# Where the pieces of the conditioning weights live during the attention: one in a place of its own, three in the turn of the projection weights

## The chip, the cores and the metric

The kernel runs on one core of one Trainium2 chip. The metric is the device time of one execution in microseconds (us). Engines are named as in the profile: PE is the matrix engine (PEld its weight loads), DVE the vector engine, ACT the scalar engine, SP the engine that issues nearly all transfers (SPq is its queue of issues). A tile of on-chip memory is named by its region: R, HL, H, I, O, P, Q, E.

## The reference, cut to what matters

Two decoder layers. Each is conditioned on a vector c: a row of 3072 numbers per layer (shift, scale and gate) comes from one product of a vector with a matrix, `ada_w`. Layer 0 has an attention over dilated windows beside a state-space part; layer 1 is a gated DeltaNet.

```python
c_act = jax.nn.silu(c)
for layer in range(DEPTH):
    mod = c_act @ ada_w[layer] + ada_b[layer]          # 1024 x 3072
    shift, scale, gate = jnp.split(mod, 3, axis=-1)
    h = rms_norm(x, pre_g[layer]) * (1.0 + scale) + shift
    y = ab_mixer(h, ...) if layer % 2 == 0 else gdn_mixer(h, ...)
    x = x + gate * rms_norm(y, post_g[layer])
...
# ab_mixer: z = h @ w_in, split into q, k, v, u, gate; attention(q, k, v) and s5(u);
#           (concatenation * silu(gate)) @ w_out
```

## The kernel before, in words

The sequence of 1024 rows stays on the chip; weights are streamed from memory in pieces of 512 KB (4 KB on each of 128 partitions). A framework of tiles inserts every wait. The part up to the end of the attention is written inside a block whose instructions a scheduler orders by a simulated timeline; from then on each engine keeps that order, so an instruction that waits holds all behind it on its engine.

The attention goes through four passes of two heads each (p = 0 to 3), each pass through eight tiles of 128 queries (t = 0 to 7). For a tile, PE makes the scores (L925, and L930 for the far keys), DVE adds the bias and finds the extremum (L943, L945, L948), ACT takes the exponential (L950), DVE divides (L951, L952), PE transposes (L965, L968, L971), ACT and DVE copy the transposes out (L966, L969, L972), and PE multiplies with the values (L978; L993 for the far keys, whose result DVE takes at L999). Between the tiles stands other work, the fillers:

- the projections of the next pass and of the gates. `load_w` takes one of three places of 4 KB, `RAW`, for a weight (SP, L291, 512 KB), splits it into a high part (ACT, L293) and a low part (DVE, L294), and 48 matmuls (L300) follow. The place comes free when the low part is made. The eight loads of the output weights (`wo`, from `ab_w_out`) go the same way in the last pass;
- eight calls of `ada`, each of which makes 512 of the numbers of `mod`. Its weight comes in four pieces of 512 KB (SP, L257), each with two matmuls (L261; the trace has two records for each). Then ACT copies the sum out to a tile `rt` (L264), PE turns it in four transposes (L246), and DVE adds up (L248, L265).

Two `ada` stand in each pass, named here by layer and column block: (0,4) and (0,5), (1,2) and (1,3), (1,0) and (1,1), (1,4) and (1,5). Before the change the pieces turn through the same three places of `RAW`, but with a counter of their own (`ada_p2`), so the first and the fourth piece of one `ada` share a place: the fourth transfer cannot be issued before the matmuls of the first have read it. `rt` lies in region E, in a pair of 2 KB places (`TMP`) that nothing else uses in the attention. `GT` is a pair of 2 KB places in P and Q that hold the tanh of a gate (ACT, L874) until DVE has used it (L876, L878).

The attention ends with the last L999; then comes the output projection of layer 0 (DVE and ACT prepare it from L1064 and L1065 on, PE multiplies at L1077).

## Time and profile before

| | |
|---|---|
| median of 3 runs | 1318.27 us (1317.27 to 1318.78) |
| profiled execution | 1327.74 us, its span 1326.0 us |
| mean granted clock of PE in it | 0.979 of full speed |
| PE busy | 94% of the span; DVE 68%, ACT 38% |
| attention in the trace | 229 to 541.5 us |

PE is busy nearly throughout, so what can be gained or lost in the attention is the time in which PE sits idle there, and the time in which its clock is granted only half. Those are read from the timeline of PE, where the idle time in front of a group of instructions stands in brackets with what ended it. The profiled execution is 9.5 us above the median of the runs.

### The profile page before, as it was taken

What the parts mean: (1) busy time and instruction counts of PE and PEld (TensorE: products, weight loads), DVE (VectorE), ACT (ScalarE), POOL (GpSimd) and SP (SyncE); (2) the same over time, 40 slices, a digit from 0 to 9 for tenths busy, and PEclk for the clock granted to TensorE, in tenths of its full rate; (3) what the DMA queues carried; (4) which work ended last, traced back from release to release, by engine and by line L of the source; (5) the groups of instructions that cost most, each with busy time, mean ns of one, the idle gap of its engine ahead of it and who ended that gap; (6) DMA issues with size and microseconds to landing.
All of it is one profiled execution on the core that took longest, in us unless ns stands there. A gap on an engine that the chain in (4) does not pass through costs nothing.

```text
span 1326.0 us, 21572 instructions
## 1 busy us (share of the span) xinstructions
PE 1241.4 (94%) x7980; PEld 952.4 (72%) x7980; DVE 903.0 (68%) x2746; ACT 505.7 (38%) x1142; POOL 23.9 (2%) x24
## 2 busy tenths in 40 slices
PE   5699999999999997899998999899999999998997
PEld 3488887856757663688765877777787778776786
DVE  7678944145252447377756978988778978988863
ACT  5462123234232335265552344423433353435421
POOL 0000000000000000000300000000000000000000
PEclk9899999999999998999998999999999999999999
DMA  9735455345051245124211122132133315255222
GB/s 315 199 93 123 121 135 158 82 120 140 0 165 55 80 124 186 69 96 133 76 32 41 48 65 81 55 88 58 57 103 81 88 48 136 76 148 182 98 87 80
DMA packets 183984, 136.62 MB, mean 103 GB/s; under 512 B 65008, under 2 KB 161629, under 8 KB 183878
## 3 DMA queue, kind: packets, MB, share of 16 engines
q1 hardware_dynamic: 167212, 124.47, 32.3%
q10 hardware_dynamic: 16586, 10.54, 2.9%
q8 instruction: 63, 1.03, 0.3%
q14 instruction: 43, 0.35, 0.1%
q0 software_dynamic: 80, 0.23, 0.0%
HBM read 107.42 MB, written 27.78 MB: 102 GB/s over the span
## 4 chain that ended last, share of the span: by engine, by line
PE 81%; DMA 7%; DVE 7%; ACT 2%; SPq 2%; issue 1%; DVEq 0%; ACTq 0%
PE psum L1275 25%; PE psum L300 14%; PE psum L1077 12%; PE psum L784 3%; PE psum L1738 2%; PE psum L1719 2%; DMA I_float<-ada_w 2%; PE psum L261 2%; PE psum L833 2%; DMA R_float<-ab_w_in 1%; DMA R_float<-ada_w 1%; PE psum L763 1%; PE psum L669 1%; DVE O_float L1305 1%; PE psum L1540 1%; PE psum L925 1%
## 5 line engine op out<-in xcount | busy, mean ns | idle before, releaser
L1275 PE MATMUL psum<-Q_float32r,HL_float32r 128*128 128x512 f32 x768 | 216.5, 416 | 6.4 <-DVE O_float L1305 3.8
L1275 PE MATMUL psum<-P_float32r,HL_float32r 128*128 128x512 f32 x768 | 210.1, 410 | 3.2 <-DVE O_float L1565 2.7
L1275 PEld LDWEIGHTS psum<-Q_float32r,HL_float32r 128*128 128x128 f32 x768 | 141.7, 194 | 37.3 <-issue 8.3
L1275 PEld LDWEIGHTS psum<-P_float32r,HL_float32r 128*128 128x128 f32 x768 | 140.7, 192 | 30.9 <-issue 3.8
L1305 DVE SCALAR_TENSOR_TENSOR O_float<-psum,vt,O_float 128x511 f32<-128x511 f32 x144 | 106.6, 740 | 1.1
L300 PE MATMUL psum<-H_float32r,HL_float32r 128*128 128x512 f32 x408 | 100.7, 397 | 2.9 <-ACT HL_float32r L293 2.9
L300 PE MATMUL psum<-I_float32r,HL_float32r 128*128 128x512 f32 x408 | 101.4, 397 | 0.0
L300 PEld LDWEIGHTS psum<-H_float32r,HL_float32r 128*128 128x128 f32 x408 | 74.9, 188 | 20.1 <-ACT HL_float32r L293 3.5
L300 PEld LDWEIGHTS psum<-I_float32r,HL_float32r 128*128 128x128 f32 x408 | 74.7, 188 | 16.9 <-issue 2.1
L1734 ACT ACTIVATE O_float<-psum,R_float 64x128 f32<-64x128 f32 x120 | 43.5, 363 | 57.2 <-DVE O_float L1725 52.9
L1310 ACT ACTIVATE E_float<-O_float 128x512 f32<-128x512 f32 x48 | 30.2, 630 | 74.1 <-DVE O_float L1305 68.6
L1077 PE MATMUL psum<-P_float32r,Q_float32r 128*128 128x512 f32 x192 | 51.9, 401 | 0.2 <-DVE Q_float32r L1065 0.2
L1756 ACT ACTIVATE O_float<-I_float 128x128 f32<-128x128 f32 x64 | 19.6, 306 | 79.9 <-DVE I_float L1755 62.3
L294 DVE TENSOR_TENSOR HL_float32r<-R_float,HL_float32r 128x1024 fp32r<-128x1024 f32 x25 | 30.5, 1221 | 28.5 <-ACT HL_float32r L293 28.4
L1725 DVE SCALAR_TENSOR_TENSOR O_float<-psum,R_float,I_float 64x128 f32<-64x128 f32 x120 | 41.7, 348 | 11.6 <-PE psum L1719 9.7
L1747 DVE SCALAR_TENSOR_TENSOR O_float<-O_float,R_float,psum 128x128 f32<-128x128 f32 x112 | 37.6, 343 | 16.4 <-PE psum L1738 9.1
L1077 PE MATMUL psum<-H_float32r,I_float32r 128*128 128x512 f32 x192 | 46.7, 390 | 1.3 <-DVE I_float32r L1065 1.3
L1738 PEld LDWEIGHTS psum<-O_float,I_float 128*128 128x128 f32 x240 | 34.4, 194 | 18.1 <-ACT O_float L1730 14.9
L1719 PEld LDWEIGHTS psum<-O_float,H_float 128*128 128x128 f32 x240 | 39.0, 193 | 10.0 <-DVE O_float L1747 2.8
L1296 ACT ACTIVATE O_float<-psum,vt 128x512 f32<-128x512 f32 x48 | 32.5, 678 | 35.7 <-PE psum L1275 35.6
L1719 PE MATMUL psum<-O_float,H_float 128*128 128x128 f32 x240 | 44.7, 288 | 1.1 <-DVE O_float L1747 1.0
L1738 PE MATMUL psum<-O_float,I_float 128*128 128x128 f32 x240 | 41.5, 294 | 3.7 <-ACT O_float L1730 3.4
(355 smaller groups left out, 2339.4 us busy)
## 6 DMA issues: line engine op xcount, KB each, us to landing
R_float<-ada_w SPq DMA_DIRECT2D x32, 512.0 KB
R_float<-gdn_w_in SPq DMA_DIRECT2D x29, 512.0 KB
R_float<-ab_w_in SPq DMA_DIRECT2D x21, 512.0 KB
I_float<-ada_w SPq DMA_DIRECT2D x8, 1024.0 KB
O_float<-x SPq DMA_DIRECT2D x8, 512.0 KB
R_float<-y_scr SPq DMA_DIRECT2D x8, 512.0 KB
R_float<-ab_w_out SPq DMA_DIRECT2D x8, 512.0 KB
R_float<-x SPq DMA_DIRECT2D x8, 512.0 KB
```

The costliest lines, as they stand in the source:

```text
L294: lo_eng.tensor_tensor(out=wh[:, 1024:2048], in0=wr, in1=wh[:, 0:1024].bitcast(F32), op=ALU.subtract)
L300: T.matmul(pj, lhsT=wh[:, sw, k, :], rhs=hT[half][:, k, sh, :], start=(k == 0 and i == 0), stop=(k == 7 and i == 2))
L784: T.matmul(pj[:, 0:256], lhsT=h4[:, k, sh_, c0:c0 + 128], rhs=wv[k // 4][:, sw, k % 4, :], start=(k == 0 and i == 0), stop=(k == 7 and i = ...
L1077: T.matmul(pb, lhsT=hl[:, so, k, :], rhs=wo[k][:, sw, 0, sl], start=(j == 0 and i == 0), stop=(j == 7 and i == 2))
L1275: T.matmul(pj, lhsT=wh[:, sw, k, :], rhs=hT[half][:, k, sh_, :], start=(n == 0), stop=(n == 23))
L1296: S.activation(t_["a"], pj, AF.Copy, scale=col("conv", 72 + b))
L1305: V.scalar_tensor_tensor(out=t_["a"][:, sl], in0=src, scalar=col("conv", 24 * i + b), in1=t_["a"][:, sl], op0=ALU.mult, op1=ALU.add)
L1719: T.matmul(psk[:, 128 * hp:128 * hp + 128], rhs=st[:, hp, :], lhsT=kq[:, c, 2 - 2 * hp:4 - 2 * hp, :].rearrange("p s i -> p (s i)"))
L1725: V.scalar_tensor_tensor(out=rt[rows], in0=psk[rows, 128 * hp:128 * hp + 128], scalar=cl["ngc"][rows, c:c + 1], in1=vc[rows], op0=ALU.mult ...
L1734: S.activation(qs[rows], psk[rows, 128 * hp:128 * hp + 128], AF.Copy, scale=egs[rows, 16 * p + c:16 * p + c + 1])
L1738: T.matmul(psu[hp], lhsT=kd[:, c % 8, hp, :], rhs=vn)
L1747: V.scalar_tensor_tensor(out=sn[:, hp, :], in0=st[:, hp, :], scalar=dec[:, hp, 16 * p + c:16 * p + c + 1], in1=psu[hp], op0=ALU.mult, op1= ...
```

## The change: what it does

The first piece of each `ada` gets region E, 4 KB, for itself. The pieces two to four are taken from `RAW` itself, by the same counter as the weights of `load_w`. Since E is taken, `rt` moves from `TMP` to the pair `GT`. No instruction is added or removed.

```diff
@@ ada
-        rt = TMP()
+        rt = GT()
         S.activation(rt, pr, AF.Copy)
...
     tables()
-    ada_p2 = Turn([p_.rearrange("p (k n) -> p k n", k=2) for p_ in RAW.places])
+    ADA_FIRST = piece(E0, 2, 512)
+    ada_i = [0]
+
+    def ada_p2():
+
+        ada_i[0] += 1
+        return RAW().rearrange("p (k n) -> p k n", k=2) if ada_i[0] % 4 != 1 else ADA_FIRST
```

The scheduler makes another order of it; the lines behind the change count seven higher. Three places.

On SP, around the start of the last pass's two `ada`. The rows with R_float<-ada_w are pieces of 512 KB, those with ab_w_out the output weights wo2 to wo7. Before:

```order
246 L257 DMA R_float_66<-ada_w 128x2x512 [waits DMAHW3_49,PE_49]
247 L291 DMA R_float_66<-ab_w_out 128x1024 [waits DMAHW2_49,PE_49]
248 L291 DMA R_float_66<-ab_w_out 128x1024 [waits DMAHW5_49,PE_49]
249 L291 DMA R_float_66<-ab_w_out 128x1024 [waits DMAHW6_49,DMAHW1_49,PE_49]
250 L291 DMA R_float_66<-ab_w_out 128x1024 [waits DMAHW7_49,DVE_49]
251 L291 DMA R_float_66<-ab_w_out 128x1024 [waits DMAHW0_49,DVE_49]
252 L291 DMA R_float_66<-ab_w_out 128x1024 [waits DMAHW4_49,DMAHW1_49,DVE_49]
253 L257 DMA R_float_66<-ada_w 128x2x512 [waits DMAHW2_49,DVE_49]
254 L257 DMA R_float_66<-ada_w 128x2x512 [waits DMAHW3_49,DVE_49]
255 L257 DMA R_float_66<-ada_w 128x2x512 [waits DMAHW4_49,DVE_49]
256 L257 DMA R_float_66<-ada_w 128x2x512 [waits DMAHW5_49,PE_49]
```

With the change:

```order
247 L257 DMA E_float_73<-ada_w 128x2x512 [waits PE_49]
248 L291 DMA R_float_66<-ab_w_out 128x1024 [waits DMAHW3_49,PE_49]
249 L291 DMA R_float_66<-ab_w_out 128x1024 [waits DMAHW6_49,PE_49]
250 L291 DMA R_float_66<-ab_w_out 128x1024 [waits DMAHW4_49,DMAHW2_49,PE_49]
251 L291 DMA R_float_66<-ab_w_out 128x1024 [waits DMAHW0_49,DVE_49]
252 L291 DMA R_float_66<-ab_w_out 128x1024 [waits DMAHW1_49,DVE_49]
253 L291 DMA R_float_66<-ab_w_out 128x1024 [waits DMAHW5_49,DMAHW2_49,DVE_49]
254 L257 DMA R_float_66<-ada_w 128x2x512 [waits DMAHW3_49,DVE_49]
255 L257 DMA R_float_66<-ada_w 128x2x512 [waits DMAHW7_49,DMAHW4_49,DVE_49]
256 L257 DMA R_float_66<-ada_w 128x2x512 [waits DMAHW5_49,DVE_49]
```

Where the fourth piece of (1,4) stood there is now the first piece of (1,5), in E, and behind the output weights stand three pieces instead of four; none of them waits for PE any more, only for DVE's low parts.

On PE, around the `ada` (1,3) of the second pass. Before:

```order
285 L261 MATMUL psum<-R_float_66,ca 32x512 x6
286 L925 MATMUL psum<-P_float_71 128x128 x2
287 L965 MATMUL psum<-cst,Q_float_1883 128x128 x4
288 L925 MATMUL psum<-P_float_71 128x256 x2
289 L968 MATMUL psum<-cst,Q_float_1883 128x128
290 L261 MATMUL psum<-R_float_66,ca 32x512 x2
291 L968 MATMUL psum<-cst,Q_float_1883 128x128
292 L978 MATMUL psum<-Q_float_1883 64x128 x4
```

With the change:

```order
291 L300 MATMUL psum<-I_float32r,HL_float32r 128x512 x2
292 L261 MATMUL psum<-E_float_73,ca 32x512 x2
293 L261 MATMUL psum<-R_float_66,ca 32x512 x6
294 L925 MATMUL psum<-P_float_71 128x128 x2
295 L971 MATMUL psum<-cst,Q_float_1883 32x128 x2
296 L246 MATMUL psum<-cst,Q_float_1883 128x128 x4
297 L925 MATMUL psum<-P_float_71 128x256 x2
298 L965 MATMUL psum<-cst,Q_float_1883 128x128 x4
```

Six matmuls, some attention and two matmuls have become one block of eight. The other five `ada` of the first three passes look the same. On SP, in front of the projection weights that follow such an `ada`, the fourth piece has given way to the first piece of the next `ada`, in E; and by their addresses in memory the weights come in another order: behind (1,3) the order was gate, q, k and is now q, k, gate, behind (0,5) it was k, gate, q and is now q, k, gate. PE multiplies with q first.

On ACT, in the last pass, from the copy of (1,4)'s sum on: L293 makes the high parts of the output weights, L966 and L950 belong to the attention's tiles t = 4 and on. Before:

```order
234 L264 ACTIVATE E_float_73<-psum 128x512
235 L966 ACTIVATE Q_float_1883<-psum 128x256
236 L293 ACTIVATE H_float32r<-R_float_66 128x1024 x2
237 L950 ACTIVATE Q_float_1883,mn<-Q_float_1883,mn 128x384
238 L966 ACTIVATE Q_float_1883<-psum 128x256 x2
239 L293 ACTIVATE H_float32r<-R_float_66 128x1024
```

With the change:

```order
237 L966 ACTIVATE Q_float_1883<-psum 128x256
238 L293 ACTIVATE H_float32r<-R_float_66 128x1024 x3
239 L966 ACTIVATE Q_float_1883<-psum 128x256 x2
240 L950 ACTIVATE Q_float_1883,mn<-Q_float_1883,mn 128x384
241 L293 ACTIVATE H_float32r<-R_float_66 128x1024
```

The high part of a third output weight (wo4) now stands ahead of the attention's two copies of the next tile.

## Rows read from the trace of the kernel before

**Rows 1.** The page: busy times, and the chain that ended last.

```profile
span 1326.0 us, 21572 instructions
PE 1241.4 (94%) x7980; PEld 952.4 (72%) x7980; DVE 903.0 (68%) x2746; ACT 505.7 (38%) x1142; POOL 23.9 (2%) x24
PE 81%; DMA 7%; DVE 7%; ACT 2%; SPq 2%; issue 1%; DVEq 0%; ACTq 0%
```

**Rows 2.** The attention, its end: length, busy PE PEld DVE ACT POOL, clock, DMA share, GB/s.

```profile
229.00:541.50 312.50, 294.07 (x2016) 195.55 (x2014) 134.26 (x499) 103.06 (x257) 0.00 (x0) 0.98 0.36 105
501.00:541.50 40.50, 30.34 (x257) 14.09 (x255) 25.45 (x92) 19.45 (x44) 0.00 (x0) 0.87 0.53 169
```

**Rows 3.** Waits of SP's queue, 215 to 545 us: total, times, longest.

```profile
SPq L257 <- PE psum L261: 135.4, 8, 40.9
```

**Rows 4.** PE's timeline, first three passes: start, length, group, idle time before it.

```profile
290.32 0.73 PE L300 MATMUL psum<-H_float32r,HL_float32r 128*128 128x512 f32 x2 [0.51 <-ACT HL_float32r L293]
...
313.35 1.05 PE L261 MATMUL psum<-R_float,ca 128*32 128x512 f32 x4 [1.63 <-DMA R_float<-ada_w]
...
316.69 0.70 PE L925 MATMUL psum<-P_float 64*128 64x256 f32 x4 [0.63 <-DVE mn L948]
...
370.12 0.66 PE L246 MATMUL psum<-cst,E_float 128*128 128x128 f32 x4 [0.22 <-ACT E_float L264]
...
385.80 1.91 PE L261 MATMUL psum<-R_float,ca 128*32 128x512 f32 x12
...
390.77 1.05 PE L261 MATMUL psum<-R_float,ca 128*32 128x512 f32 x4 [1.06 <-DMA R_float<-ada_w]
...
396.79 0.73 PE L300 MATMUL psum<-H_float32r,HL_float32r 128*128 128x512 f32 x2 [1.02 <-ACT HL_float32r L293]
...
439.70 1.91 PE L261 MATMUL psum<-R_float,ca 128*32 128x512 f32 x12
...
445.06 1.05 PE L261 MATMUL psum<-R_float,ca 128*32 128x512 f32 x4 [0.29 <-DMA R_float<-ada_w]
...
447.91 1.06 PE L300 MATMUL psum<-H_float32r,HL_float32r 128*128 128x512 f32 x2 [1.32 <-ACT HL_float32r L293]
...
469.90 1.05 PE L261 MATMUL psum<-R_float,ca 128*32 128x512 f32 x4 [0.92 <-DMA R_float<-ada_w]
```

**Rows 5.** SP's issues beside `ada` (1,3) and beside (1,0).

```profile
386.89 0.37 SPq L257 DMA_DIRECT2D R_float<-ada_w  x1
387.37 4.86 SPq L291 DMA_DIRECT2D R_float<-ab_w_in  x3
440.80 0.37 SPq L257 DMA_DIRECT2D R_float<-ada_w  x1
441.26 0.42 SPq L291 DMA_DIRECT2D R_float<-ab_w_in  x1
```

**Rows 6.** PE's timeline, last pass: groups behind a wait.

```profile
507.72 1.05 PE L261 MATMUL psum<-R_float,ca 128*32 128x512 f32 x4 [1.45 <-DMA R_float<-ada_w]
...
520.58 0.47 PE L968 MATMUL psum<-cst,Q_float 128*128 128x128 f32 x1 [3.01 <-ACT Q_float L966]
...
532.77 1.30 PE L261 MATMUL psum<-R_float,ca 128*32 128x512 f32 x4 [3.19 <-DMA R_float<-ada_w]
```

**Rows 7.** The chain from 500 to 543 us: start, length, what.

```profile
514.52 4.66 DMA R_float<-ab_w_out
...
527.78 4.95 DMA R_float<-ada_w
```

**Rows 8.** Stretches of the last pass, columns as in group 2.

```profile
510.00:520.00 10.00, 5.60 (x66) 3.21 (x66) 9.56 (x31) 6.23 (x11) 0.00 (x0) 0.99 0.62 205
520.00:522.00 2.00, 1.42 (x5) 1.01 (x7) 1.43 (x2) 1.42 (x3) 0.00 (x0) 0.50 0.71 224
```

**Rows 9.** ACT's timeline, last pass: high parts of wo4 and wo7.

```profile
513.47 1.05 ACT L293 ACTIVATE H_float32r<-R_float 128x1024 fp32r<-128x1024 f32 x1
...
521.11 1.06 ACT L293 ACTIVATE I_float32r<-R_float 128x1024 fp32r<-128x1024 f32 x1 [0.58 <-DMA R_float<-ab_w_out]
```

## The prediction

> **What bounds the kernel now.** I read the page first: PE is busy 94% of the span, and 81% of the chain that ended last is PE's own work, 7% transfers [rows 1]. So the whole kernel is bound by PE, and an edit that moves no work off PE can gain only where PE sits idle. The change touches the attention alone, so next come the stages: in the attention PE is busy 294.07 of 312.50 us, which leaves 18.4 us idle, and 10.2 of these lie in the last 40.5 us, where the clock is also lowest, 0.87 in the mean [rows 2]. Then who is waited for. In SP's queue the eight issues of an `ada` piece that wait for the matmuls of an earlier piece stand first, 135.4 us in sum [rows 3]. That is no loss by itself, since SP has nothing better to do; it says that a place comes free late. PE's timeline shows where it hurts. Each `ada` starts with three pieces present, and the fourth is issued only when the first has been read. PE fills the time with attention, and where that runs out it waits: 1.63, 1.06, 0.29 and 0.92 us in the first three passes [rows 4], 1.45 and 3.19 in the last [rows 6]. Behind these come waits for the high part of the next projection weight, 0.51, 1.02 and 1.32, and an after-effect of 0.63 through DVE [rows 4]. The last pass is another regime: from 510 to 520 us DVE is busy 9.56 of 10 us while PE does 5.60, and just after it PE's granted clock is 0.50, the 1.2 GHz level [rows 8].
>
> **The change part by part.** Work added or removed: none, the same transfers, matmuls and copies. `rt` in `GT` instead of `TMP` is the same copy; it could delay the next tanh of a gate by having the place still occupied, but two places turn and the transposes that free it follow within a few attention groups; the nearest row, a transposition that waited for the copy, is 0.22 us [rows 4]. I take 0, with 0 to 1 us for all eight.
>
> *The second `ada` of passes 0 to 2* ((0,5), (1,3), (1,1)). Now all four pieces have places before the `ada` starts, because the last one needs only a low part that DVE made long before. The wait for the fourth piece goes: 1.63, 1.06 and 0.92, and the after-effect 0.63. What is late next is the projection weight. Take (1,3): it starts at 385.80; the fourth piece went out at 386.89 and the first weights from 387.37 [rows 4, 5]. With the change the piece in E goes out at the same point, since it too waits for the first piece's matmuls, and the weights follow at A + 1.57 as before (A is the start of the `ada`). How long do they take? At (1,0) a weight was issued at 441.26 behind a fourth piece at 440.80 [rows 5]; its L300 starts at 447.91, straight after a high part of 1.06 us [rows 4, 9], so it landed near 446.8, 5.5 us after issue. With that the weight of (1,3) lands at A + 7.1 and its high part is ready at A + 8.2. PE's own work up to L300 there is 396.79 - 385.80 less the two waits of 1.06 and 1.02, so 8.9 us. It fits: both waits go, provided that the weight that PE wants comes first, and the new order has q first where the old one had the gate's. At (1,1) likewise. At (0,5) PE's new order reaches L300 earlier, after about 7.5 us by adding up its groups, an estimate, so some 0.7 us come back. Gain: 1.63 + 0.63 + 1.06 + 1.02 + 0.92 - 0.7 = 4.6 us; bounds 2 (weights some 1 us later at each) and 5.3 (no wait comes back).
>
> *The first `ada`* ((0,4), (1,2), (1,0)). Before, three pieces and a late fourth also; the waits are 0.51 at (0,4), 0.22 at (1,2), and 0.29 + 1.32 at (1,0) [rows 4]: 2.3 us. At (1,0) L300 came at 447.91 - 439.70 = 8.2 us after the start, of which 1.6 were waits, so 6.6 of work. In the new order the four transposes L246, 0.66 us, stand ahead of L300: 7.3 of work against the same 8.2 for piece in E and weight. Wait 0.95. At (1,2) the same sum with somewhat more attention gives 0.5; at (0,4) the new order has less cover, about 6.9 us, and I take 1.3. Sum 2.75: a loss of 0.45 us. Bounds: a gain of 2.3, a loss of 3.
>
> *The last pass*, counted on the chain. Before, the fourth piece of (1,5) is issued at 527.78, lands after 4.95 us [rows 7], PE starts on it at 532.77 after 3.19 us of nothing [rows 6], and the attention ends at 541.5, 8.7 us later [rows 2]. Now the three pieces in R wait only for the low parts of wo5, wo6 and wo7. The last of these: high part from 521.11 for 1.06 [rows 9], low part about as long again, so 523.3. The last piece goes out then and not at 527.78: 4.5 us earlier. It lands at 528.2, and the same 8.7 us end at 537. Some of what stands before it moves too: the wait of 1.45 for the fourth piece of (1,4) goes, since that piece is issued ahead of need. But that opens onto the stretch that DVE fills (9.56 of 10), so I give it only 0.5. Against it stands the order on ACT: the high part of wo4 stands ahead of the two copies of tile 4, and those of wo6 and wo7 ahead of tile 5's. wo4's starts at 513.47, wo7's at 521.11, so a copy may come a high part (1.06) later, twice; I do not count it in the chain, because the pieces' places hang on just these weights and come no later for it. Sum: 5.0 us gained; bounds 0 (DVE and the output weights' transfers, 4.66 us each [rows 7], fix the end) and 9 (most of the 10.2 idle us).
>
> *Start of the attention.* The first piece in E is issued ahead of the small transfer for the bias tables. Its region has been read by then, so no new wait; a share of the bandwidth: 0.5 us lost, 0 to 1.
>
> *Output projection of layer 0.* Its order changes slightly on every engine, by no change of work; PE has its matmuls in hand there. 0, within 2 either way.
>
> Sum: -4.6 + 0.45 - 5.0 + 0.5 = -8.65 us. The durations come from the profiled execution of 1327.74 us, which is 9.5 above the median of the runs, 1318.27; I take the difference over unscaled: 1318.27 - 8.65 = **1309.6 us**.
>
> **A rule weighed against it.** Near the last pair the transfers run at 169 GB/s in the mean, and at 205 from 510 to 520 [rows 2, 8], so 524 KB occupy them some 2.6 us. The Trainium skill, page "DMA: Bandwidth & Descriptors", section "Issuing engines are not separate DMA queues", says that all transfers end up on the same 16 engines and interleave. By that rule a piece in a place of its own brings no bandwidth of its own, and put ahead of a weight it only makes the weight later; the trace agrees that weights behind a piece take longer than the piece itself (5.5 against 3.9 us). By the rule alone the sum would be that of the third rival below; by the rows it is not, because a piece stood at the same spot before.
>
> **The rivals.** *The last pass gives nothing.* DVE's 9.56 of 10 us and the chain of output weights fix when the attention can end; the piece comes earlier and PE waits at L966's copies instead, as it did for 3.01 us at 520.58 [rows 6]. For it: that wait is as long as the one that goes. Against: the 3.19 us stand at the end, when DVE is nearly done. Then -4.6 + 0.45 + 0.5 = -3.65, 1314.6 us.
>
> *Nothing is gained.* Every wait for the fourth piece turns into one for the next weight, the cover being shorter now that the eight matmuls stand in a block, and the last pass gives its gain back at the weights' high parts ahead of the attention on ACT. 1318 us, within 2.6.
>
> *Slower: the piece in E holds up the weights.* If it truly comes on top, each of the six blocks in passes 0 to 2 waits 2.6 us at L300: 15.6, less the 7.6 that these passes wait now (5.3 + 2.3), and the last pass and the start still give 4.5: +3.5, 1321.8 us. It decides once the wait is above (7.6 + 4.5 + 2.6)/6 = 2.45 us per block. Against it: the fourth piece was issued at 386.89, 0.5 us ahead of the weights [rows 5], so one piece is replaced by one. For it: the cover is 7 to 9 us, and the weight's arrival is not much below that.
>
> **How the numbers follow.** Forecast (gain of 5 to 15 us) 0.58; last pass gives nothing 0.19; nothing gained 0.11; slower 0.12. A measurement of this kernel tells 0.2%, 2.6 us, from no change. Faster 0.58 + 0.19 = 0.77, same 0.11, slower 0.12. The best case: 5.3 + 2.3 in the first passes and 7 of the 9 in the last would be -14.6, about 1303.5; I set the low end there. The high end takes in the second rival and half of the one without gain, 1319.5; what lies beyond is the slower case and a little of the best one.
>
> **What would show it.** Right: L261's waits for ada_w gone in passes 0 to 2 and the eight matmuls in one stretch; waits at L300 of 0.5 to 1.3 us behind (0,4), (1,2), (1,0) and (0,5), none behind (1,3) and (1,1); the last piece of (1,5) issued some 2 us after wo7's high part starts, and not 6.7 us after it (527.78 - 521.11); the attention ending some 8 us earlier. Wrong, if waits of 2 us or more stand at L300, or if PE waits in the last pass for L966 or for output weights as long as it did for ada_w. The forecast would also fail if the granted clock fell to 0.5 more often, since every 2 us at that level do the work of one.

## The result, and the profile after

| | before | after |
|---|---|---|
| median, first comparison | 1318.15 us (6 runs, 1317.27 to 1319.38) | 1313.63 us (6 runs, 1310.44 to 1315.29) |
| median, second comparison | 1322.12 us (23 runs) | 1315.97 us (5 runs) |
| ratio with its 95% interval | | 0.9947 [0.9932, 0.9962], then 0.9961 [0.9948, 0.9974] |
| profiled execution | 1327.74 us | 1314.91 us |

The change makes the kernel faster by 0.4 to 0.5%. The ratios come with their intervals from the comparison by rounds and are not quotients of the medians; as times they are 7.0 and 5.2 us, the two differences of medians 4.5 and 6.2 us. All four lie below the forecast gain of 8.65 us, so about half to four fifths of it came.

The forecast was made on one profiled execution of before, which lay at the long end of what this kernel does. So each of the two kernels was profiled twice, and below both traces of each are used: the first of before (span 1326.0 us), a second (1316.9 us), and two of after (1313.1 and 1314.0 us).

The page of the kernel after answers to [rows 1]: the span, the busy times, and the chain that ended last.

```profile
span 1313.1 us, 21589 instructions
PE 1236.1 (94%) x7980; PEld 951.1 (72%) x7980; DVE 903.8 (69%) x2746; ACT 506.4 (39%) x1142; POOL 23.4 (2%) x24
PE 83%; DVE 6%; DMA 6%; ACT 2%; SPq 2%; issue 1%; DVEq 0%; ACTq 0%
```

The kernel is bound as before. PE's idle time, the span less its busy time, is 77.0 us where it was 84.6. In the second trace of before it is 81.6 (1316.9 - 1235.3), in the second of after 77.9. The stretches tell where. Columns are those of [rows 2]: length, busy PE, PEld, DVE, ACT, POOL, clock, DMA share, GB/s. In the first trace of after, the first line is the first three passes, from the start of (0,4) to the start of (1,4); the second is the last pass, from there to the first full group of the output projection's matmuls; then come three stretches used further down.

```profile
276.03:495.43 219.40, 214.03 (x1529) 145.36 (x1528) 96.73 (x367) 72.74 (x187) 0.00 (x0) 0.98 0.33 97
495.43:532.55 37.12, 28.34 (x257) 12.87 (x256) 25.86 (x94) 19.68 (x44) 0.00 (x0) 0.91 0.55 186
...
442.00:448.00 6.00, 5.57 (x34) 2.92 (x34) 3.17 (x12) 2.17 (x7) 0.00 (x0) 0.50 0.52 157
505.00:515.00 10.00, 5.90 (x64) 3.22 (x63) 10.00 (x29) 7.41 (x12) 0.00 (x0) 0.94 0.67 225
514.00:520.00 6.00, 5.19 (x20) 1.82 (x20) 3.63 (x12) 1.94 (x6) 0.00 (x0) 0.50 0.67 231
```

The same two stretches in the first trace of before, cut at the same instructions:

```profile
277.63:501.11 223.48, 215.21 (x1529) 144.10 (x1528) 96.48 (x367) 71.76 (x187) 0.00 (x0) 0.99 0.32 96
501.11:542.71 41.60, 30.23 (x256) 14.09 (x255) 26.55 (x94) 19.40 (x44) 0.00 (x0) 0.88 0.53 173
```

In the second trace of before:

```profile
277.38:499.46 222.08, 213.92 (x1529) 143.51 (x1528) 96.21 (x367) 71.64 (x187) 0.00 (x0) 1.00 0.32 96
499.46:538.69 39.23, 28.69 (x256) 12.94 (x256) 26.45 (x94) 19.56 (x44) 0.00 (x0) 0.91 0.58 183
```

And in the second of after:

```profile
277.37:495.46 218.09, 212.73 (x1529) 144.49 (x1528) 96.58 (x367) 72.91 (x187) 0.00 (x0) 0.99 0.33 98
495.46:534.30 38.84, 29.59 (x256) 13.47 (x255) 26.00 (x94) 19.53 (x44) 0.00 (x0) 0.87 0.56 178
```

Read length less PE busy, the idle time. In the passes it is 8.27 and 8.16 us before, 5.37 and 5.36 after: 2.85 us less. In the last pass it is 11.37 and 10.54 before, 8.78 and 9.25 after: 1.94 less. The lengths fall by 4.0 (from 222.8 to 218.7 in the mean) and by 2.4 (from 40.4 to 38.0).

In the passes, then, PE's busy time fell as well, by 1.2 us, though its granted clock is lower after. The clock is at 0.50 for 3.4 us in the first trace of before (from 448.12), never in the second, and for 6.8 and 3.4 us after (from 442.05 and from 443.99). In such a stretch half of PE's busy time is lost, an estimate from the clock: 1.7 us and nothing before, 3.2 and 1.7 after. So at full clock the work fell by about 2.8 us. The matmuls of the pieces show where. Their own busy time in the passes (the first number behind the length is now that of L261 alone), in the first trace of before and of after:

```profile
277.63:501.11 223.48, 18.76 (x97) 3.33 (x97) 0.99 0.32 96
276.03:495.43 219.40, 12.58 (x97) 2.63 (x97) 0.98 0.33 97
```

The second traces have 18.81 and 12.58. It is 6.2 us less for the same matmuls, about 1.0 for each `ada`. Before, six of them took 1.91 us and the last two 1.05 by themselves [rows 4]; now the eight of (1,3) take 1.9 us together:

```profile
382.90 0.62 PE L261 MATMUL psum<-E_float,ca 128*32 128x512 f32 x2
382.92 0.62 PE L261 MATMUL psum<-R_float,ca 128*32 128x512 f32 x2
...
383.37 1.46 PE L261 MATMUL psum<-R_float,ca 128*32 128x512 f32 x10
```

Those of the piece in E and of the next one, in R, start within 0.02 us of each other and run at the same time. The kernel puts four in a row into four different places of the result (`g4 = 32 * (k % 4)` and `tile_position=(0, g4)` at L261). So the last two, standing alone, took as long as four. At (0,4) one matmul still stands apart, at 280.05, so that `ada` does not look quite like the others. The rest of PE's work took some 3 us more in the new order at full clock; why is not shown.

What the change was to remove, it removed. What L261 itself waited for, over the whole program, in us and times, first in before and then after (PE and its weight loads are counted side by side, so one wait can stand there twice):

```profile
  DMA R_float<-ada_w: 20.2, 16
...
  DMA E_float<-ada_w: 2.4, 2
  DMA R_float<-ada_w: 0.9, 2
```

SP still waits for L261, 121.5 us where [rows 3] had 135.4. After, all four waits of L261 stand in the last pass. In the passes no `ada` waits for a piece any more. PE's timeline of after, against [rows 4] and [rows 6], shows what it waits for instead:

```profile
309.28 0.73 PE L300 MATMUL psum<-H_float32r,HL_float32r 128*128 128x512 f32 x2 [0.54 <-ACT HL_float32r L293]
...
367.65 0.74 PE L300 MATMUL psum<-H_float32r,HL_float32r 128*128 128x512 f32 x2 [1.36 <-ACT HL_float32r L293]
...
442.44 1.22 PE L300 MATMUL psum<-H_float32r,HL_float32r 128*128 128x512 f32 x2 [2.08 <-ACT HL_float32r L293]
...
468.49 0.73 PE L300 MATMUL psum<-H_float32r,HL_float32r 128*128 128x512 f32 x2 [0.20 <-ACT HL_float32r L293]
...
512.26 0.44 PE L965 MATMUL psum<-cst,Q_float 128*128 128x128 f32 x2 [1.17 <-DVE Q_float L952]
...
514.25 0.48 PE L968 MATMUL psum<-cst,Q_float 128*128 128x128 f32 x1 [1.55 <-ACT Q_float L966]
...
515.71 1.92 PE L261 MATMUL psum<-R_float,ca 128*32 128x512 f32 x4 [0.55 <-DMA R_float<-ada_w]
...
526.21 0.44 PE L965 MATMUL psum<-cst,Q_float 128*128 128x128 f32 x2 [0.66 <-DVE Q_float L972]
```

The first four stand behind (0,5), (1,2), (1,0) and (1,1): the wait is now for the high part of the weight that follows. Behind the 2.08 us PE's granted clock is 0.50, the 1.2 GHz level, from 442 to 448 (window above). In the last pass the 3.19 us of [rows 6] have become 0.55. PE waits for DVE and ACT in the middle about as long as before, and behind the last piece there are new waits for them, 0.66 here and 1.16 us in sum.

### The profile page after: what moved, and what is told of

The parts are those of the page before. It is cut to its first block, busy times and chain, and to the rows that moved or that the text cites. A ratio compares the mean times of both kernels' runs of the same rounds, so it can differ in the third digit from the quotient of the medians.

```text
span 1313.1 us, 21589 instructions
## 1 busy us (share of the span) xinstructions
PE 1236.1 (94%) x7980; PEld 951.1 (72%) x7980; DVE 903.8 (69%) x2746; ACT 506.4 (39%) x1142; POOL 23.4 (2%) x24
## 3 DMA queue, kind: packets, MB, share of 16 engines
q10 hardware_dynamic: 16586, 10.54, 3.0%
q8 instruction: 63, 1.03, 0.3%
## 4 chain that ended last, share of the span: by engine, by line
PE 83%; DVE 6%; DMA 6%; ACT 2%; SPq 2%; issue 1%; DVEq 0%; ACTq 0%
PE psum L1282 26%; PE psum L300 15%; PE psum L1084 12%; PE psum L784 4%; PE psum L1745 2%; PE psum L1726 2%; DMA I_float<-ada_w 2%; PE psum L833 2%; DMA R_float<-ab_w_in 2%; PE psum L763 1%; PE psum L669 1%; PE psum L1547 1%; PE psum L261 1%; DVE O_float L1312 1%; PE psum L925 1%; PE psum L978 1%
## 5 line engine op out<-in xcount | busy, mean ns | idle before, releaser
L1282 PEld LDWEIGHTS psum<-Q_float32r,HL_float32r 128*128 128x128 f32 x768 | 141.2, 194 | 37.2 <-issue 8.3
L300 PE MATMUL psum<-H_float32r,HL_float32r 128*128 128x512 f32 x408 | 102.2, 400 | 4.2 <-ACT HL_float32r L293 4.2
L300 PE MATMUL psum<-I_float32r,HL_float32r 128*128 128x512 f32 x408 | 101.9, 398 | 0.0
L300 PEld LDWEIGHTS psum<-H_float32r,HL_float32r 128*128 128x128 f32 x408 | 75.1, 189 | 22.7 <-ACT HL_float32r L293 5.2
L300 PEld LDWEIGHTS psum<-I_float32r,HL_float32r 128*128 128x128 f32 x408 | 75.1, 189 | 17.3 <-issue 2.4
L950 ACT ACTIVATE Q_float<-Q_float,mn 128x128 f32<-128x128 f32 (+7 forms) x64 | 35.7, 560 | 22.4 <-DVE mn L945 12.6
```

The source lines that it names most:

```text
L300: T.matmul(pj, lhsT=wh[:, sw, k, :], rhs=hT[half][:, k, sh, :], start=(k == 0 and i == 0), stop=(k == 7 and i == 2))
L950: S.activation(pm[:, c0:c1], pm[:, c0:c1], AF.Exp, scale=-1.0, bias=mn[:, 1:2], accum_out=mn[:, 2:3])
L1282: T.matmul(pj, lhsT=wh[:, sw, k, :], rhs=hT[half][:, k, sh_, :], start=(n == 0), stop=(n == 23))
```

## The experiments

There are two questions: why waits came back at L300 in the passes, and why the last pass gave less than half of what was forecast. The theories are named in the expectations. Each trace is one execution; ratios are to the kernel before on the same chip.

**The kernel before and the kernel after once more**, without an edit.

> The kernel before, unchanged, for a second trace beside the first one, which was 9.5 us above the median of its runs. Time by both theories 1318 us. First theory (the profiled execution of before was long outside the attention): from the start of (0,4) to the first full matmul group of the output projection again about 265 us. Rival (it was long in the attention, by more time at the half clock or longer waits for transfers): 4 us or more shorter there, and then the gain that the two traces show in the attention, 8.5 us, is larger than what a typical pair of runs shows.

Measured 0.9996 [0.9978, 1.0014]; 10 runs lie between 1317.7 and 1327.5 us, and the 35 runs of before beside it between 1316.7 and 1327.1, with a mean granted clock from 0.986 at the short end to 0.977 at the long one. So one kernel alone spreads over 10 us, with the clock, and the first profiled execution was at the long end. From the start of (0,4) to the first full group of the output projection it took 265.1 us in the first trace and takes 261.3 in the second. So 3.8 of the 9.1 us between their spans lie there, close to the rival's 4, and 5.1 lie behind it.

> The changed kernel, unchanged, beside the kernel before on one chip, since the runs of one kernel spread over 10 us in the first set. First theory (the gain is real and comes from the waits for the fourth piece): 0.3 to 0.4% below before; in the trace no wait of L261 for a piece in passes 0 to 2, waits at L300 of 1 to 2 us behind (1,2) and (1,0), followed by a stretch at the half clock. Rival (the two parts alone gave 0.1% each, so the whole gives 0.2% and the rest was the spread of the runs): 0.1 to 0.2% below.

Measured 0.9961 [0.9948, 0.9974], as the first theory had it. The waits stand where they stood: 0.63, 1.35 and 1.89 us at L300 for the 0.54, 1.36 and 2.08 of the first trace.

**The new scheme in the first three passes only, and in the last pass only.**

```diff
-        rt = GT()
+        rt = GT() if not (l == 1 and n >= 4) else TMP()
...
-        return [lambda n=n: ada(l, ada_p2, 2, n) for n in ns]
+        return [lambda n=n: ada(l, ada_p2 if not (l == 1 and n >= 4) else ada_own, 2, n) for n in ns]
```

`ada_own` is a turn with the counter of before. The second kernel has the condition the other way round.

> The change for the six ada of passes 0 to 2 alone; (1,4) and (1,5) take their pieces and their copy as before. First theory (the gain has two parts, the first passes and the last): about half of the gain of 4.5 us, 1315 to 1317. Rival (the last pass gives nothing, DVE and the output weights fix its end): the whole gain, 1313 to 1314.

> The change for (1,4) and (1,5) alone. First theory (two parts): 1315 to 1317. Rival (the last pass gives nothing): 1318, within 0.2% of before.

Measured 0.9989 [0.9971, 1.0008] for the first and 0.9989 [0.9975, 1.0003] for the second: neither part alone can be told from no change, and together they would be 0.2%, less than the 0.4 to 0.5% of the whole. A reason is in PE's timeline of the passes-only kernel, behind (1,1):

```profile
467.72 0.73 PE L300 MATMUL psum<-H_float32r,HL_float32r 128*128 128x512 f32 x2 [2.61 <-ACT HL_float32r L293]
```

Where after waits 0.20, this kernel waits 2.61. Its (1,1) starts at 460.57 and reaches L300 at 467.72, after 7.15 us; after takes from 459.99 to 468.49, 8.50. The scheduler has put L300 further forward, though against the kernel after nothing is edited in this pass. So the parts can't be added up: an edit in one pass moves work in another. The passes' length was 222.08 us, as in before, not 218.7.

The last-pass-only kernel shows a second reason. Its last pass, and the stretch in it in which the clock is granted half:

```profile
498.79:537.85 39.06, 29.75 (x256) 13.35 (x255) 26.00 (x94) 19.59 (x44) 0.00 (x0) 0.83 0.54 180
512.95:526.60 13.65, 9.88 (x50) 3.33 (x46) 8.72 (x27) 5.55 (x11) 0.00 (x0) 0.50 0.59 190
```

It is 39.06 us long, about as before. Half of the 9.88 us that PE is busy at 0.50 is lost there. Without that loss, an estimate, the pass would be 34.1 us, as in after, where before comes to 36.9 and 36.3: in this execution the clock took what the edit gave.

**Only the place of its own, and only the shared turn.** The first keeps the piece in E and lets the other three turn by the counter of before (edit against after); the second has no piece in E and takes all four from `RAW` (edit against before).

```diff
-        return RAW().rearrange("p (k n) -> p k n", k=2) if ada_i[0] % 4 != 1 else ADA_FIRST
+        return ada_own() if ada_i[0] % 4 != 1 else ADA_FIRST
```

```diff
-    ada_p2 = Turn([p_.rearrange("p (k n) -> p k n", k=2) for p_ in RAW.places])
+    def ada_p2():
+        return RAW().rearrange("p (k n) -> p k n", k=2)
```

> The first piece in E, but the other three turn through the three places of R with a counter of their own, as before. First theory (what counts is that no piece shares a place with an earlier piece of the same ada): as the changed kernel within 2 us. Rival (the common counter counts, since a piece and a weight then never ask for the same place at once): about as the kernel before, with L300 waiting for weights whose place a piece still holds.

> No place in E: all four pieces from the turn of the weights, three places. First theory: the fourth piece still takes the place of the first, so the waits of 1 to 1.6 us for it stay, and the time is that of before within 0.2%. Rival (the common counter counts): 0.2 to 0.4% below before.

Measured 0.9994 [0.9979, 1.001] and 0.9981 [0.9968, 0.9995]. The place of its own, which I held to be the whole cause, gives nothing measurable alone. It does remove the waits for pieces in the passes, and L261 takes 12.58 us there as in after, but behind (1,0) the weight comes later. SP's queue beside (1,0) in this kernel:

```profile
441.77 0.37 SPq L257 DMA_DIRECT2D E_float<-ada_w  x1
442.23 0.93 SPq L257 DMA_DIRECT2D R_float<-ada_w  x2
443.26 0.42 SPq L291 DMA_DIRECT2D R_float<-ab_w_in  x1
```

and PE's timeline behind it:

```profile
452.34 0.73 PE L300 MATMUL psum<-H_float32r,HL_float32r 128*128 128x512 f32 x2 [2.40 <-ACT HL_float32r L293]
```

The same stretch of SP's queue in the kernel after:

```profile
435.46 0.37 SPq L257 DMA_DIRECT2D E_float<-ada_w  x1
435.93 0.41 SPq L291 DMA_DIRECT2D R_float<-ab_w_in  x1
```

At this place, with two counters, two more pieces stand between the piece in E and the first weight; with a common one the weight is second. Three pieces ahead of a weight cost 2.40 us here, the size that the rival "slower" gave to one. Two more waits are as long, 2.03 us at 475.49 and 2.54 at 394.30 (there through ACT, where a high part that waits for its weight stands ahead of an exponential), but at both only the piece in E stands ahead of the first weight, as in after. So further pieces are not their reason; behind (1,1) PE has 6.8 us of work in front of L300, where after has 8.0. Each of the three waits is followed by a stretch at the granted clock 0.50, 6.8 us behind the one at 394.30 and 3.4 us behind each of the others. The passes of this kernel:

```profile
277.49:503.58 226.09, 216.49 (x1529) 148.21 (x1528) 95.60 (x367) 73.46 (x187) 0.00 (x0) 0.97 0.32 94
```

They are 3.3 us longer than before.

The shared turn alone still waits for the fourth piece, 0.70 and 1.03 us, and yet takes 0.2%. Both halves are needed for the whole gain. In its one trace the passes take 221.03 us and the last pass 37.05, as short as in after; whether the shared turn is enough there, one trace can't tell, since the two of before differ by 2.4 us.

**The piece in E behind the weights.** The issue of the first piece is held in program order, except for (0,4) and (1,5).

```diff
-            SY.dma_start(wt, A["ada_w"]...)
+            ld = SY.dma_start(wt, A["ada_w"]...)
+            if k0 == 0 and (l, n) not in ((0, 4), (1, 5)):
+                tc.keep_in_program_order(ld)
```

> The changed kernel, with the piece in E issued behind the next projection weights instead of ahead of them, for all ada but (0,4) and (1,5). First theory (the piece in E delays the weight behind it, and PE pays at L300, 1.36 and 2.08 us behind (1,2) and (1,0), with some us at the half clock after the longer one): these waits fall below 0.5 us, and the time falls 2.5 to 5 us below the changed kernel's, to 1309 to 1311. Rival (the weight is late by its own transfer, not by the piece): the waits stay within 0.3 us and the time stays at 1313 to 1314.

Measured 0.9999 [0.9984, 1.0015], so the gain is lost. The profiled execution is the longest of its 12. PE's timeline, line numbers two higher: behind (1,3) first, where after had no wait at L300, and then behind (1,0).

```profile
392.82 0.73 PE L302 MATMUL psum<-H_float32r,HL_float32r 128*128 128x512 f32 x2 [1.47 <-ACT HL_float32r L295]
...
447.75 0.97 PE L302 MATMUL psum<-H_float32r,HL_float32r 128*128 128x512 f32 x3 [0.42 <-DVE HL_float32r L296]
```

Behind (1,0) the wait fell from 2.08 to 0.42. But others came up, 1.00 us behind (0,4), 1.76 behind (1,1) and the 1.47 behind (1,3). That `ada` starts at 386.51 here, so 6.3 us pass to L302, of which 4.8 are work; in after 8.2 us pass, of which 7.9 are work. The weight was issued at 387.64, 1.1 us behind the start where after has 1.6, and landed after 3.99 us. It came sooner, and the scheduler put its consumer sooner still. My theory that the weight's arrival alone sets the wait fell: the consumer's place in the order counts as much. That the wait is the distance between the simulated arrival, by which the order is made, and the real one is argued from this; the simulated arrival was not read.

**The order of PE held.** The first matmul of each projection half in the attention stays in program order, so that no consumer moves forward.

```diff
-                T.matmul(pj, lhsT=wh[:, sw, k, :], rhs=hT[half][:, k, sh, :], ...)
+                mm = T.matmul(pj, lhsT=wh[:, sw, k, :], rhs=hT[half][:, k, sh, :], ...)
+                if pin and k == 0 and i == 0:
+                    tc.keep_in_program_order(mm)
```

> The changed kernel with the first matmul of each half of a projection in the attention kept behind what is written ahead of it in the program, so that it cannot be moved forward to where its weight has only just been asked for. First theory (the waits at L300 arise because the new order puts L300 6 to 8 us behind the start of an ada, and a weight needs 5.5 us from issue plus 1.1 for its high part): they fall below 0.3 us each and the time 2 to 5 us below the changed kernel's. Rival (moving L300 back uncovers other waits of the attention, for DVE and ACT, which the order had hidden): the waits at L300 go, as many us come back at L965, L968 and L925, and the time is that of the changed kernel or above.

Measured 1.0162 [1.0148, 1.0176]. Most waits for weights did go (one of 1.25 us is left behind (1,1)), but the edit takes away other cover. PE at the start of the attention:

```profile
262.25 0.47 PE L969 MATMUL psum<-cst,Q_float 128*128 128x128 f32 x1 [12.68 <-DMA Q_float<-b_scr]
```

The bias tables' transfer had been covered by projections that are now kept behind it. The first pass begins at 298.38 for about 277; the three passes took 219.93 us, which is 1.2 more than after. The experiment was meant to isolate one wait and made another, so it says little on the first.

**The fourth place in the common turn**, instead of for the first piece alone.

```diff
-    ADA_FIRST = piece(E0, 2, 512)
+    RAW = Turn(RAW.places + [piece(E0, 1024)])
```

> E not kept for the first piece but put into the turn as a fourth place, for weights and pieces alike; the weight behind an ada then goes out ahead of the next piece, into the place that the first piece leaves. First theory (what counts is four places in one turn; which transfer uses which is not important): within 2 us of the changed kernel, 0.2 to 0.5% below before, with waits at L300 of 1 to 2 us still there, because the order puts L300 earlier when the weight goes out earlier. Rival (the order of piece and weight is what costs the 1.4 and 2 us at L300): these two waits fall below 0.5 us, and the time is 2 to 5 us below the changed kernel's.

Measured 1.0039 [1.0025, 1.0054]. A wait at the start of the attention and one behind (1,3):

```profile
227.67 1.22 PE L300 MATMUL psum<-H_float32r,HL_float32r 128*128 128x512 f32 x2 [3.50 <-ACT HL_float32r L293]
...
399.60 0.73 PE L300 MATMUL psum<-H_float32r,HL_float32r 128*128 128x512 f32 x2 [1.51 <-ACT HL_float32r L293]
```

A fourth place for all does not help. Up to (0,4) PE is idle for 36.2 us, where it was 27 to 28 in before and after, and behind the second `ada` of each pass L300 waits 1.5 to 1.7 us.

**The last pass: DVE relieved.** Three low parts of output weights on GpSimd.

```diff
-        wo[k] = load_w(..., dst=wo_dst[k])
+        wo[k] = load_w(..., dst=wo_dst[k], lo_eng=G if k in (3, 5, 7) else V)
```

> The changed kernel with the low parts of wo3, wo5 and wo7 made by GpSimd instead of DVE, which takes 3.7 us off DVE in the stretch of the last pass in which DVE is busy all the time. First theory (DVE's order, not the last piece of (1,5), fixes the end of the last pass now): from the start of (1,4) to the first full group of the output projection 34 to 36 us, where the two traces of the changed kernel show 37.1 and 38.8, and a time 1.5 to 4 us below the changed kernel's, 0.5 to 0.7% below before. Rival (the transfers of the output weights fix it, each waiting for the place of an earlier one): GpSimd, at some 2.4 us for a low part, gives the places back later, the wo transfers and the last piece come 1 to 3 us later, and the time is the changed kernel's or 1 to 3 us above.

Measured 0.9942 [0.9923, 0.9961], the best ratio of all, but not to be told from after's. Windows of this kernel, the last pass and its middle:

```profile
495.07:532.68 37.61, 27.27 (x256) 12.70 (x256) 25.94 (x91) 19.59 (x44) 7.34 (x3) 0.95 0.58 185
...
505.00:515.00 10.00, 6.40 (x63) 3.32 (x63) 7.93 (x28) 6.43 (x12) 4.76 (x2) 0.84 0.57 174
```

DVE falls from 10.00 to 7.93 of 10 us, and the pass stays at 37.61 against 37.12 and 38.84. Some of the waits move to the pieces; PE's timeline:

```profile
523.91 1.05 PE L261 MATMUL psum<-R_float,ca 128*32 128x512 f32 x4 [1.29 <-DMA R_float<-ada_w]
```

**The last pass: (1,5) ahead of the output weights**, alone and with the edit above.

```diff
-             gate_fill(3) + gate_fill(7) + [lambda: wo_load(0), lambda: wo_load(1)] + ada_fill(1, (4,)) +
-             [lambda k=k: wo_load(k) for k in range(2, 8)] + ada_fill(1, (5,))]
+             gate_fill(3) + gate_fill(7) + [lambda: wo_load(0), lambda: wo_load(1)] + ada_fill(1, (4, 5)) +
+             [lambda k=k: wo_load(k) for k in range(2, 8)]]
```

> The changed kernel with (1,5) written straight behind (1,4), ahead of wo2 to wo7. The last transfers of the attention are then output weights, on which PE does not wait inside it. First theory (DVE with its low parts fixes the end): DVE's work is the same, only its last weights come later; the end of the last pass stays within 1 us, 37 to 39 us after the start of (1,4), and the time within 2 us of the changed kernel's. Rival (the late pieces of (1,5) still fix it): 2 to 4 us less.

> The two edits of the last pass together: (1,5) written ahead of wo2 to wo7, and the low parts of wo3, wo5 and wo7 on GpSimd. First theory (in the last pass of the changed kernel two chains end at nearly the same time, the pieces of (1,5) and DVE's work on the output weights, so relieving one alone gives nothing there): from the start of (1,4) to the first full group of the output projection 34 to 36 us, where the changed kernel had 37.1 and 38.8, and 0.6 to 0.8% below before. Rival (the transfers of the output weights alone fix the end, in whatever order): 37 to 39 us, and 0.3 to 0.5% below before.

Measured 0.9975 [0.996, 0.999] and 0.9951 [0.9933, 0.9968]. PE's timeline of the first of them:

```profile
523.62 0.69 PE L965 MATMUL psum<-cst,Q_float 128*128 128x128 f32 x2 [3.02 <-DVE Q_float L952]
```

and of the second a window near the end, and then its whole last pass:

```profile
522.00:532.00 10.00, 7.70 (x57) 5.04 (x54) 4.84 (x14) 4.35 (x9) 4.87 (x2) 0.50 0.36 114
...
494.75:533.23 38.48, 30.39 (x257) 14.97 (x256) 26.18 (x90) 19.06 (x44) 10.13 (x4) 0.82 0.61 194
```

With the pieces out of the way a wait of 3.02 us stands at DVE, and the pass takes 39.59 us. With DVE relieved too, the pass is still 38.48 us, and PE works ten microseconds at 1.2 GHz. My theory that the end is set by two chains, the pieces and DVE, so that removing both gains what neither gives, fell by its own numbers. The rival's numbers, 37 to 39 us and 0.3 to 0.5%, were met by the edits together. But its reason, the transfers of the output weights, is not shown: no run takes these transfers away. What the traces do show is the clock. With half of PE's busy time at 0.50 taken off, the same estimate as above, the pass is 34.2 and 34.1 us in the traces of after, 33.7 with the pieces moved alone, 32.9 with both edits and 36.0 with DVE alone relieved. So with the pieces moved the pass would be 0.5 to 1.3 us shorter than after's, but it spends 17.1 and 13.7 us at 1.2 GHz, where after has 6.8 and 10.2. With DVE alone relieved it is the waits: PE's idle time is 10.34 us for 8.78 and 9.25.

## Why the prediction was right, and where its sizes were off

The direction and the range held. The gain came out smaller, and by its median of 1313.63 the result lies nearer the rival by which the last pass gives nothing (1314.6) than the forecast (1309.6). By the mechanism neither is exact: the last pass did give something, about half.

*Work added or removed: none.* This term was put at nothing, and it was wrong. The instructions are the same, but PE's time for the matmuls of the pieces in the passes fell from 18.8 to 12.6 us, since the eight run in one block. The forecast named the block; that it shortens the cover stood in a rival, and no term priced either.

*The second `ada` of the passes.* The waits for the fourth piece went, with the after-effect through DVE, as forecast. Of those that were to come back, (0,5) got 0.54 (forecast 0.7), (1,3) none at L300, (1,1) 0.20 (forecast none), and 0.30 and 0.31 stand at transpositions beside these two. Right in the mechanism and nearly in size.

*The first `ada`.* This term was mis-sized. Forecast waits: 1.3 at (0,4), 0.5 at (1,2), 0.95 at (1,0), 2.75 in sum. Measured: none at L300 behind (0,4), 1.36 and 2.08, in sum 3.44, and 0.52 at an attention transposition beside (0,4). That is some 0.7 to 1.2 us more than forecast. Behind (1,0) the weight was no later than forecast: L300 starts 8.07 us behind the start of the `ada`, where the sum had 8.2. What was mis-sized is the work in front of it, 7.3 us in the sum and 6.0 measured. The same attention groups stand there in both orders, and the four transposes as forecast; but the sum kept the 1.05 us of the fourth piece's two matmuls, which in the block cost almost nothing. At (1,2) the work is 6.5 us where the forecast needed 7.7; there the new order also puts the next tile's scores behind L300. So the joined block, a gain in PE's work, is what shortened the cover.

The two terms for the passes together were -4.15 us. The length fell by 4.0, and that this is so near is luck: the waits gave 2.85, PE's work at full clock about 2.8, which had no term, and the granted clock took back about 1.6. The forecast was of waits, so the idle time is the fairer measure. One kernel's two traces differ by 1.3 to 1.4 us in this length.

*The last pass* is the step that was most off: forecast 5.0, measured 2.4. The issue came as forecast. The three issues of (1,5) begin at 511.84 and take 3.87 us together, so the last came at about 515.3, some 2.4 us behind the start of wo7's high part at 512.87, where the forecast said 2 and before had 6.7. Forecast was that PE starts on it 27.1 us into the pass (528.2 - 501.1); in the first trace of after it starts at 522.78, 27.35 us in, in the second 29.1. Before it was 31.7 and 30.8. So this is 3.0 us in the mean where I had 4.5, and the 0.5 for the earlier pieces of (1,4) did not come: the pieces at 499.16 and 502.00 wait 0.37 and 1.08 us, where before had 0.17 and 1.45. Then "the same 8.7 us end at 537". The chain of after from the issue on (start, length, what; some groups left out):

```profile
511.84 3.73 DMA R_float<-ada_w
...
515.71 1.92 PE psum L261 x4
...
519.09 1.72 PE psum L261 x4
...
522.85 1.01 PE psum L261 x4
...
523.88 0.60 ACT Q_float L264
524.48 0.66 ACT Q_float L950 x2
```

From the last piece's matmuls to the end it is 9.77 and 9.76 us after (522.78 to 532.55, 524.54 to 534.30). In before it was 9.94, of which 3.4 us at a granted clock of 0.50, and 8.46 in the second trace, at 1.00. The copy of the sum (L264) now stands ahead of two exponentials on ACT, and PE waits for what follows from them, 1.16 us in the first trace and 1.15 in the second. And the path was another than the one forecast: PE does not wait for the last piece at all, it reaches it by its own work behind the first of the three, and in the first trace of after this runs at 1.2 GHz from 514 to 520. So some 2.8 us of waiting for pieces at the end of the pass went, and 1.16 us of new waits came behind them. The clock is not the difference. By the same estimate, half of PE's busy time at 0.50, it takes 4.7 and 2.9 us of the last pass before, 2.9 and 4.7 after. Without that the pass would be 36.9 and 36.3 before and 34.2 and 34.1 after, again 2.4 gained. What else holds the end is open; the experiments on the last pass did not settle it.

*DVE in the middle.* I gave the earlier pieces of (1,4) only 0.5 because they open onto a stretch that DVE fills. It does: 10.00 of 10 us from 505 to 515 ([rows 8] had 9.56), with PE waiting 1.17 and 1.55 us for DVE and ACT there, 0.61 and 2.56 in the second trace. The rival "the last pass gives nothing" was right in what it named, and wrong in that it takes all.

*Start of the attention and output projection.* Up to the start of the attention PE's idle time is 27.8 and 28.0 us before, 27.2 and 28.0 after, and none from there to (0,4). The 0.5 us for the piece ahead of the bias tables did not show. From the end of the attention on it is 37.2 and 34.9 before, 35.7 and 35.3 after: no change outside the spread of one kernel.

*The rule against the change*, that all transfers interleave on the same 16 engines, is of the Trainium skill, page "DMA: Bandwidth & Descriptors", section "Issuing engines are not separate DMA queues". In this kernel one piece replaced one, and the waits stayed below the 2.45 us per block from which that rival would have decided. At the one place where a run puts three pieces ahead of a weight, the trace agrees with it: there the wait is 2.40 us.

*The signs.* Two signs of a wrong forecast were met in part. A wait of 2 us stands at L300, at one of six places: 2.08 and 1.89 us behind (1,0). And the granted clock was at 0.50 for longer in the passes, 6.8 and 3.4 us after for 3.4 and none before. The output projection's first full group began 10.2 and 4.4 us earlier, trace against trace, for the 8 forecast for the end of the attention.

*Numbers.* The difference was taken over unscaled from an execution 9.5 us above the median. In the passes that did no harm: idle time differs by 3.0 us between the two traces of before, 2.3 of it behind the attention, where the change does nothing, and in the passes by 0.1. In the last pass it did: that pass is 41.6 us in the first trace and 39.2 in the second, and the wait that was to go is 3.19 in one and 2.27 in the other. What stays open is the split between the passes and the last pass in time rather than in idle time, since the kernels with one part alone are also ordered otherwise.

## What to carry to other kernels

Where a scheduler orders consumers by a simulated arrival, an earlier transfer shortens a wait only if the consumer stays where it is; count the work in front of the consumer in the new order, not in the old one. And when an edit brings instructions together, ask whether they now run at the same time: the same count of instructions need not be the same work. When two streams share buffers, look at who stands between a freed place and the transfer that is needed first: here a common counter was as necessary as the additional place. Profile the unchanged kernel twice before a difference of half a per cent is explained line by line.

## What was unexpected in the hardware

Eight matmuls of 32 rows of result each took 1.9 us in one block and 2.96 us as six and two, with the same instructions; four of them run at the same time.

Some short waits cost more than their length. The waits of 2.08 and 1.89 us behind (1,0) in the two traces of after were followed by 6.8 and 3.4 us at a granted clock of 0.50, and the wait of 1.32 us there in the first trace of before by 3.4 us. In the second trace of before, with a wait of 1.22 us at the same place, the passes ran at 1.00 in the mean, and so did the kernel with the shared turn alone, with waits of 1.33 and 1.32.

512 KB took between 3.73 us (a piece at 511.84 in after) and 6.26 us (an output weight at 496.98 in the same trace), and 3.99 for a weight in the kernel that sends weights first. A low part on GpSimd took 2.36 to 2.58 us in the kernel with DVE relieved, against 1.22 on DVE; this still did not lengthen the last pass measurably.
